# VectorE instead of GpSimd for every fourth weight subtraction in a two-block transformer kernel

## The chip, the cores and the metric

The kernel runs on one core of a Trainium2 chip. The metric is the device time of one execution in microseconds (us), taken as the median of several runs. The profile comes from one further execution, recorded by the hardware profiler.

## The reference

The input x is 256 tokens by 1024 features, in float32. Two blocks run one after the other.

- **First block.** `h = rms_norm(x)`, a projection `h @ w_in` of three kinds of attention (banded and dilated, sliding window with sinks, stick-breaking) and three gates, then `merged = sum of sigmoid(gate) * (o @ w_branch)`, `@ w_out`, a norm and a residual. After it a feed-forward part: `u = h @ w_up` (1024 to 8192), a causal convolution over three tokens, `gelu(gate) * val`, `@ w_down`, norm, residual.
- **Second block, two layers.** Each modulates a norm of x (and of a context of 256 tokens, in layer 0 to the end, in layer 1 only as far as attention needs it) with vectors `c_act @ ada_w`; projects with `w_in`; runs a chunked state-space scan (SSD) and a differential attention; merges both through `w_ssd_o`, `w_attn_o` and `w_out`; and adds `square(relu(h @ w1)) @ w2`, the MLP. A last norm ends it.

Nearly all arithmetic is in products of the form `h @ W` with 256 or 512 tokens, and all weights are float32.

## The kernel before

**Pieces.** Every weight matrix comes to SBUF in pieces of 128 partitions by 1024 float32 values (512 KB), each used for eight 128-row slices of one block of columns. `wload` (L194 to L214) handles one piece in three steps. A DMA on SyncE's queue brings it into `wr` (L202). ScalarE copies it to the reduced float32 format of TensorE, which gives its high part `wh` (L210). A subtraction gives the low part, `wl = wr - wh` (L213):

```python
nc.scalar.activation(hi, raw, AF.Copy)
self.nsplit += 1
eng = nc.gpsimd if self.nsplit % self.pool_every == 0 else nc.vector
eng.tensor_tensor(lo, raw, hi.bitcast(F32), op=ALU.subtract)
```

`nsplit` counts the pieces; `pool_every` is set stage by stage from the table `pv` or from constants: 4 in the first block, 8 for the SSD stages, 99 (next to none) in differential attention and one stretch of the MLP, 4 elsewhere. There are 578 pieces; 112 of the subtractions fall to GpSimd and 466 to VectorE.

**Products.** Activations are split into a high and a low part in the same way (`split`, L257; `h` of a modulated norm, L949). `mmT` (L220 to L232) then does three matmuls for each slice: L230 is high by high, L231 high by low, L232 the low part of the weight by the high part of the activation; `mmN` (L251 to L253) does the same with the operands exchanged. The slot of `wr` comes free when both parts have been made, the slots of `wh` (five) and `wl` (five) when the matmuls have read them.

**What sets the order.** TensorE's instructions run in the order in which the program writes them (`in_order`); generators are woven by hand, so that projections fill the gaps of attention or the scan. On the other engines a tile scheduler sets the order by priorities, before the run; each engine then takes its instructions strictly in that order and waits at the first whose operand isn't there. `wload` gives its three steps a priority that depends on when earlier pieces are used.

**Other names.** `sq` (L303) are sums of squares in `norm`. `rstd` turns them into the inverse root: VectorE's `rv` (L272), GpSimd's `rr` (L274), VectorE's diagonal `dg` (L278); TensorE spreads that over the partitions (L286, `sm`) and the norm is multiplied in on VectorE (L946). `acc` (L830) on VectorE is a tap of the convolution in the feed-forward part, it reads PSUM; `gv` (L835) on GpSimd is its gated product. L915 on VectorE are the dot products of the modulation vectors, with raw weights `wa` from the same buffers as `wr`. L1748 on VectorE adds a branch to the residual.

Of the kernel before, what the change touches and what calls it, by code (L numbers as in the profile page):

```python
# [10 lines left out]
F32 = mybir.dt.float32  # L11
F32R = mybir.dt.float32r
AF = mybir.ActivationFunctionType
ALU = mybir.AluOpType
# [84 lines left out]
class Net:  # L99
    def __init__(self, ctx, tc, A, stop=None, x_only=False):  # L100
        self.ctx, self.tc, self.nc, self.A = ctx, tc, tc.nc, A
        self.stop = stop
        p = lambda name, bufs, **k: ctx.enter_context(tc.tile_pool(name=name, bufs=bufs, **k))
        self.cp = p("cp", 1)
        self.NR, self.NH = 6, 5
        self.back = 4
        self.wr = p("wr", self.NR)
        self.wh = p("wh", self.NH)
        self.wl = p("wl", 5)
        self.ps_mm = p("psmm", 3, space=PSUM)  # L110
        self.ps_sm = p("pssm", 3, space=PSUM)
        self.ps_lg = p("pslg", 2, space=PSUM)
        self.sp = p("sp", 2)
        self.nsplit = 0
        self.HP = 100
        self.MW = 2
        self.H2 = 256
        self.XP = (1,3,5)
        self.GN = 4
        self.RP = 100  # L120
        self.pieces = []
        self.first = None
        self.pv = (4,4,4,8,99,4,4)
        self.pool_every = self.pv[0]
        self.FD = ({2:(0,),4:(1,),6:(2,),7:(3,)},{2:(0,),4:(1,),7:(2,3)})
        self.B0 = (5,5)
        self.WW = ((2,0,1),(2,0,2))
        self.NA = 12
        self.L = (3,2)
        self.L0 = (4,4)  # L130
        nc = self.nc
        self.cst = self.cp.tile([P, 6 * P], F32, name="cst")
        self.smt = self.cp.tile([P, NSM], F32, name="smt")
        self.row = self.cp.tile([P, NRW], F32, name="row")
        self.nhalf = self.cp.tile([P, 4], F32, name="nhalf")
        nc.vector.memset(self.nhalf, -0.5)
        warm = self.cp.tile([P, 4], F32, name="warm")
        nc.scalar.activation(warm, self.nhalf, AF.Copy)
# [55 lines left out]
    def wload(self, src, kt=8, eng=None):  # L194


        nc = self.nc
        shape = [P, kt, src.shape[1] // kt]
        now = self.tc.tile_snap_priority()
        with self.tc.high_priority(offset=0 if self.first is None else min(self.RP, max(0, now - self.first))):  # L200
            raw = self.wr.tile(shape, F32, tag="wr", name="wr")
            (eng or nc.sync).dma_start(raw, src.rearrange("p (k n) -> p k n", k=kt))  # L202

        turn = self.pieces[-self.back][0] if len(self.pieces) >= self.back else 0
        piece = [now]
        self.pieces.append(piece)
        with self.tc.high_priority(offset=0 if self.first is None else max(0, min(now - 1, now - turn))):
            hi = self.wh.tile(shape, F32R, tag="wh", name="wh")
            lo = self.wl.tile(shape, F32R, tag="wl", name="wl")
            nc.scalar.activation(hi, raw, AF.Copy)  # L210
            self.nsplit += 1
            eng = nc.gpsimd if self.nsplit % self.pool_every == 0 else nc.vector
            eng.tensor_tensor(lo, raw, hi.bitcast(F32), op=ALU.subtract)  # L213
        return [(hi[:, k, :], lo[:, k, :], piece) for k in range(kt)]  # L214

    def wload2(self, src):
# [124 lines left out]
    def first_block(self, es_x):  # L341


        nc, tc, A = self.nc, self.tc, self.A
        w_in = A["w_in"]
        xsrc = lambda k: A["xT"][k * P:(k + 1) * P, :]
        with ExitStack() as es:
# [410 lines left out]
            def context():  # L758
                for _ in range(8):
                    yield  # L760
                yield from self.mod_norm(0, 0, 1, xc, hc, 0, t1, nc.gpsimd if 1 else None)
                for k in range(8):
                    nc.sync.dma_start(hcd[k], hct[k].bitcast(F32))
# [8 lines left out]
            W2 = A["w_in_2"][0]  # L772
            with self.in_order():
                self.ada_finish(0, 0, 24)
                self.pool_every = self.pv[1]
                bg = [context()]
                self.weave(merge(), bg)
                self.weave(project(), bg)
                self.dump("d_hs", hs)

                free = []

                def t16():
                    if not free:
                        for c in range(4, 12):
                            t = pb.tile([P, 2, 256], F32, tag=f"gate{c}", name="t16")
                            free.extend((t[:, 0, :], t[:, 1, :]))
                    return free.pop(0)

                bg = [self.add_normed(x, hs, "post_g", t16)]  # L790
                self.step(bg)
                self.weave(self.gate_blocks(W2[72:76], hc, 0, 256, spill(t1)), bg)
                while bg:
                    self.step(bg)
                h = self.pairs(po, 8, 256, "o")
                bg = [self.normed(x, "ffn_g", t16, h)]
                self.step(bg)
                sink = spill(t1)
                self.weave(self.gate_blocks(W2[76:80], hc, 0, 256, lambda i, make: sink(4 + i, make)), bg)
                while bg:  # L800
                    self.step(bg)

        self.hp = self.side_pool(es_x, "hp", 8, "left")
        with ExitStack() as es:
# [41 lines left out]
                    else:  # L846
                        nc.vector.tensor_tensor(hs[c], pv_, hs[c], op=ALU.add)

            self.pool_every = self.pv[2]
            with self.in_order():  # L850
                for q in range(4):
                    mid = self.pairs(pm, 8, 256, "mid")
# [203 lines left out]
    def ssd_open(self, l, h):  # L1056

        class Phase:
            pass

        class Tags:
            def __init__(s_):
                s_.m = {}

            def tile(s_, shape, dt, tag, name):
                return s_.m[tag].tile(shape, dt, tag=tag, name=name)

        nc = self.nc
        S = Phase()
        S.es, S.tags, S.bg, S.times, S.fr, S.h = ExitStack(), Tags(), [], {}, {}, h  # L1070
        S.p4 = self.side_pool(S.es, f"s4{l}", 4, "right")
        S.p2 = self.side_pool(S.es, f"s2{l}", 3, "right")
        S.tags.m.update({"cv": S.p4, "bc": S.p4, "sz": S.p4, "s2": S.p2})
        p1 = self.side_pool(S.es, f"sc{l}", 1, "right")
        self.cwh = p1.tile([P, 160], F32, name="cwh")
        nc.vector.tensor_scalar(self.cwh, self.sm(f"cw{l}"), 0.5, None, op0=ALU.mult)
        self.cbh = p1.tile([P, 32], F32, name="cbh")
        nc.vector.tensor_scalar(self.cbh, self.sm(f"cb{l}"), 0.5, None, op0=ALU.mult)
        S.dT = S.p2.tile([64, 512], F32, tag="s2", name="dT")
        self.pool_every = (4,4)[l]  # L1080
        S.nv = (3,2)[l]
        S.vd = self.tc.dram_tile([S.nv, P, 512], F32, name=f"vd{l}")
        S.front = self.ssd_front(l, 0, h, S.fr, S.tags, S.dT, lambda: S.bg.append(S.start()))
        return S
# [377 lines left out]
    def layer(self, l, x, S):  # L1462

        nc, tc, A = self.nc, self.tc, self.A
# [2 lines left out]
        nt = T // P  # L1467
        W = A["w_in_2"][l]
        h = S.h
        self.pool_every = (8,8)[l]  # L1470
        yd = tc.dram_tile([16, P, T], F32, name=f"yd{l}")
        ad = tc.dram_tile([8, P, T], F32, name=f"ad{l}")
        gd = tc.dram_tile([8, P, T], F32, name="gd1") if last else self.gd
# [8 lines left out]
        with S.es as es:  # L1482
# [11 lines left out]
            fr, front = S.fr, S.front  # L1494
            for g in range(8):
                self.weave(front, bg)
                self.pool_every = self.pv[3]
                bg.append(self.ssd_back(l, g, fr, S.times, yd, ssq, pools))
                if g < 7:
                    fr = {}  # L1500
                    front = self.ssd_front(l, g + 1, h, fr, S.tags)
# [7 lines left out]
            while bg:  # L1509
                self.step(bg)  # L1510
        nc.vector.tensor_reduce(tot[:, :nt], ssq[:, :nt, :], axis=AX.X, op=ALU.add)
        self.pool_every = self.pv[4]
        es_m, es_x, es_p, es_g = ExitStack(), ExitStack(), ExitStack(), ExitStack()
        pg = pool(es_g, "g", 8, "right")
        gs = []
# [28 lines left out]
            while bg:  # L1544
                self.step(bg)
        pt = pool(es_m, "mt", 6, "left")
        self.pool_every = self.pv[5]
        px = pool(es_x, "xc", 1, "left")
        streams = [(0, x, 0)]
        if not last:  # L1550
# [14 lines left out]
        with self.in_order():  # L1565
# [51 lines left out]
            if last:  # L1617
                es_g.close()
                pr = pool(es_g, "raw", 1, "right")
                raw = [pr.tile([P, 2, 258], F32R, name=f"raw{k}") for k in range(8)]  # L1620
                raw = [(t[:, 0, :], t[:, 1, :]) for t in raw]
# [7 lines left out]
        if not last:  # L1629
            es_g.close()  # L1630
        es_p.close()
        self.pool_every = self.pv[6]
        with ExitStack() as es, self.in_order():
            pma = pool(es, "ma", 8, "left")
            es_e = ExitStack()
# [55 lines left out]
            if last:  # L1691
                self.step(bg)
                self.weave(up_raw(), bg)
                es_g.close()
            else:

                self.weave(up(0, range(4), 256, 512), bg)
                self.pool_every = 99
                self.weave(up(1, range(4), 256, 512), bg)
                while bg:  # L1700
                    self.step(bg)
                bg.append(adas())
                self.weave(up(0, range(4), 0, 256), bg)
                self.pool_every = self.pv[6]
            for e in range(1, 7):
                cols = (0, 256) if e == 1 and not last else (0, T)
                self.weave(up(e, range(2), *cols), bg)
# [166 lines left out]
```

## Time and profile before

| what | value |
|---|---|
| median of 3 runs | 2613.73 us |
| lowest and highest | 2606.41 and 2618.48 us |
| the profiled execution, its own time | 2611.19 us |
| its span in the trace | 2609.4 us |
| mean granted TensorE clock | 0.991 of full speed |

The span lies between the first and the last instruction that the trace shows; 1.8 us of the profiled execution's time lie around it. The engines are PE (TensorE's matmuls), PEld (its weight loads), DVE (VectorE), ACT (ScalarE), POOL (GpSimd) and SP (SyncE, which issues most DMAs). Of an engine that isn't the bottleneck, idle time costs nothing by itself.

### The profile page before, as it was taken

Reading aid. Unit: us, or ns where it says so; the run is one execution under the profiler, and the core shown is the slowest. Engines: PE = TensorE matmul, PEld = TensorE weight load, DVE = VectorE, ACT = ScalarE, POOL = GpSimd, SP = SyncE. Lnnn points to the kernel's source line nnn. Section 1 sums busy time; section 2 is a strip of 40 time slices with the busy share of each in tenths; the row PEclk is TensorE's granted clock in tenths of the full one; section 3 lists DMA queues with packets and bytes.
Section 4 is the critical chain, followed back from the end, with each engine's and each line's share of the span. In section 5 each row is a group of like instructions: output and inputs, shape, how many; then the busy total and the mean of one; then the engine's idle time right before and its main releaser. Section 6 shows DMA issues by size and latency. Waiting matters only on the chain.

```text
span 2609.4 us, 44555 instructions
## 1 busy us (share of the span) xinstructions
PE 2513.0 (96%) x16698; PEld 2263.5 (87%) x16698; DVE 1876.7 (72%) x2990; ACT 1423.7 (55%) x2722; POOL 875.5 (34%) x757
## 2 busy tenths in 40 slices
PE   7999899999999999999999899999999999999998
PEld 7899899998888888888879878789878888899998
DVE  7887776877577765777796886636777767778664
ACT  5654565564656564666434623335565546665654
POOL 3123533332455564210133311014365542212321
PEclk9999899999999999999999999999999999999999
DMA  7665665663434335322674556624444343355552
GB/s 258 219 222 206 205 214 183 209 218 131 140 121 130 127 120 167 107 95 75 221 255 138 195 193 232 203 97 146 150 142 135 114 160 132 104 189 201 171 186 98
DMA packets 179766, 431.27 MB, mean 165 GB/s; under 512 B 18884, under 2 KB 84610, under 8 KB 179294
## 3 DMA queue, kind: packets, MB, share of 16 engines
q1 hardware_dynamic: 176254, 424.26, 48.6%
q0 software_dynamic: 2720, 3.64, 0.5%
q8 instruction: 132, 2.16, 0.3%
q14 instruction: 84, 0.69, 0.1%
q10 hardware_dynamic: 576, 0.52, 0.1%
HBM read 406.82 MB, written 18.32 MB: 163 GB/s over the span
## 4 chain that ended last, share of the span: by engine, by line
PE 57%; DVE 14%; DMA 8%; issue 7%; POOL 6%; ACT 6%; SPq 1%; POOLq 0%; DVEq 0%; ACTq 0%
PE mm L230 14%; PE mm L231 14%; PE mm L232 14%; DMA wa<-in_adaT_dram 4%; DVE wl L213 3%; PE mm L251 2%; PE mm L252 2%; PE mm L253 2%; DVE th L915 2%; ACT wh L210 2%; DVE junk L915 1%; PE sm L1190 1%; PE sm L1266 1%; POOL E L1175 1%; PE sm L1253 1%
## 5 line engine op out<-in xcount | busy, mean ns | idle before, releaser
L210 ACT ACTIVATE wh<-wr 128x1024 fp32r<-128x1024 f32 x578 | 610.1, 1057 | 631.1 <-PE mm L231 487.7
L230 PE MATMUL mm<-h,wh 128*128 128x256 f32 (+1 forms) x2232 | 765.7, 343 | 16.7 <-ACT r L1648 7.0
L213 DVE TENSOR_TENSOR wl<-wr,wh 128x1024 fp32r<-128x1024 f32 x466 | 603.9, 1298 | 223.2 <-ACT wh L210 216.9
L231 PE MATMUL mm<-h,wh 128*128 128x256 f32 (+1 forms) x2232 | 744.5, 334 | 2.6 <-DVE h L949 1.4
L232 PE MATMUL mm<-h,wl 128*128 128x256 f32 (+1 forms) x2232 | 744.7, 334 | 0.0
L213 POOL TENSOR_TENSOR wl<-wr,wh 128x1024 fp32r<-128x1024 f32 x112 | 285.6, 2550 | 796.1 <-ACT wh L210 734.0
L230 PEld LDWEIGHTS mm<-h,wh 128*128 128x128 f32 x2232 | 422.4, 189 | 67.7 <-ACT r L1648 7.2
L231 PEld LDWEIGHTS mm<-h,wh 128*128 128x128 f32 x2232 | 422.5, 189 | 51.9 <-issue 5.7
L232 PEld LDWEIGHTS mm<-h,wl 128*128 128x128 f32 x2232 | 421.8, 189 | 43.1
L230 PE MATMUL mm<-mid,wh 128*128 128x256 f32 (+1 forms) x832 | 254.9, 306 | 4.3 <-DVE xc L1748 3.9
L231 PE MATMUL mm<-mid,wh 128*128 128x256 f32 (+1 forms) x832 | 254.9, 306 | 1.4 <-DVE mid L257 1.3
L232 PE MATMUL mm<-mid,wl 128*128 128x256 f32 (+1 forms) x832 | 254.4, 306 | 0.0
L251 PE MATMUL mm<-wh,h 128*128 128x256 f32 (+1 forms) x704 | 202.3, 287 | 2.6 <-DVE bc L1051 1.2
L252 PE MATMUL mm<-wl,h 128*128 128x256 f32 (+1 forms) x704 | 197.1, 280 | 0.0
L253 PE MATMUL mm<-wh,h 128*128 128x256 f32 (+1 forms) x704 | 197.0, 280 | 0.0
L230 PE MATMUL mm<-o,wh 128*128 128x256 f32 x592 | 168.0, 284 | 13.0 <-ACT wh L210 7.7
L230 PEld LDWEIGHTS mm<-mid,wh 128*128 128x128 f32 x832 | 156.8, 188 | 14.5 <-issue 4.5
L232 PE MATMUL mm<-o,wl 128*128 128x256 f32 x592 | 167.6, 283 | 0.9 <-DVE wl L213 0.9
L231 PE MATMUL mm<-o,wh 128*128 128x256 f32 x592 | 167.2, 282 | 0.0
L231 PEld LDWEIGHTS mm<-mid,wh 128*128 128x128 f32 x832 | 156.6, 188 | 10.1 <-DVE mid L257 2.0
L232 PEld LDWEIGHTS mm<-mid,wl 128*128 128x128 f32 x832 | 156.4, 188 | 8.2
L915 DVE SCALAR_TENSOR_TENSOR th<-wa,cb 128x1024 bf16<-128x1024 f32 x96 | 136.7, 1432 | 12.8 <-DMA wa<-in_adaT_dram 11.9
(373 smaller groups left out, 4960.9 us busy)
## 6 DMA issues: line engine op xcount, KB each, us to landing
wr<-in_w_in_dram SPq DMA_DIRECT2D x247, 512.0 KB, 3.6
wr<-in_w_mlp_dram SPq DMA_DIRECT2D x144, 512.0 KB, 4.2
wa<-in_adaT_dram SPq DMA_DIRECT2D x96, 512.0 KB, 4.4
wr<-in_w_up_dram SPq DMA_DIRECT2D x64, 512.0 KB, 4.3
wr<-in_w_out_dram SPq DMA_DIRECT2D x32, 512.0 KB, 3.5
wr<-in_w_down_dram SPq DMA_DIRECT2D x32, 512.0 KB, 4.2
wr<-in_w_ssd_o_dram SPq DMA_DIRECT2D x32, 512.0 KB, 3.7
E<-csd SPq DMA_DIRECT2D x24, 512.0 KB, 4.4
```

The lines of the kernel that those rows point to most:

```text
L210: nc.scalar.activation(hi, raw, AF.Copy)
L213: eng.tensor_tensor(lo, raw, hi.bitcast(F32), op=ALU.subtract)
L230: nc.tensor.matmul(ps, wh, xh, start=start and k == 0, stop=False)
L231: nc.tensor.matmul(ps, wh, xl, start=False, stop=False)
L232: nc.tensor.matmul(ps, wl, xh, start=False, stop=stop and k == n - 1)
L251: nc.tensor.matmul(ps, xh, wh, start=k == 0, stop=False)
L252: nc.tensor.matmul(ps, xh, wl, start=False, stop=False)
L253: nc.tensor.matmul(ps, xl, wh, start=False, stop=k == n - 1)
L915: nc.vector.scalar_tensor_tensor(junk, raw, 0.5, self.cb[:, s, :], op0=ALU.mult, op1=ALU.mult, accum_out=self.mods[l][:, 2 * i + m, s:s + 1])
L1175: nc.gpsimd.tensor_tensor(v, v, t, op=ALU.add)
L1190: nc.tensor.matmul(ps[:, d0:d1, :], BN[:, c, :], xw[:, d0:d1].rearrange("p d h e -> p d (h e)"), start=True, stop=True)
L1253: nc.tensor.matmul(ps[:, d0:d0 + n].rearrange("p d h e -> p d (h e)"), C[:, ck * P:(ck + 1) * P], H[ck][:, d0:d0 + n, :], start=True, stop ...
```

## The change

The choice of the engine goes. The subtraction of L213 is always VectorE's, and `nsplit`, `pool_every` and `pv` are removed everywhere. Line numbers after the change are lower by 5 to 15 (L213 is then L208, L278 is L273, L835 is L829, L830 is L824, L949 is L942, L1748 is L1733).

```diff
-        self.nsplit = 0
...
-        self.pv = (4,4,4,8,99,4,4)
-        self.pool_every = self.pv[0]
...
             nc.scalar.activation(hi, raw, AF.Copy)
-            self.nsplit += 1
-            eng = nc.gpsimd if self.nsplit % self.pool_every == 0 else nc.vector
-            eng.tensor_tensor(lo, raw, hi.bitcast(F32), op=ALU.subtract)
+            nc.vector.tensor_tensor(lo, raw, hi.bitcast(F32), op=ALU.subtract)
...
-                self.pool_every = self.pv[1]
...
-            self.pool_every = self.pv[2]
...
-        self.pool_every = (4,4)[l]
...
-        self.pool_every = (8,8)[l]
...
-                self.pool_every = self.pv[3]
...
-        self.pool_every = self.pv[4]
...
-        self.pool_every = self.pv[5]
...
-        self.pool_every = self.pv[6]
...
-                self.pool_every = 99
...
-                self.pool_every = self.pv[6]
```

TensorE's order is the same. On the other engines the scheduler places things anew. Three places show how.

The first is VectorE's queue in the norm ahead of the MLP of layer 0, between the residual's updates (`xl`) and the first modulated activations (`nt`, `h`). Before:

```order
L213 TENSOR_TENSOR wl<-wr,wh 128x1024
L1748 SCALAR_TENSOR_TENSOR xl_2746<-mm,mod_86,xl_2746 128x256
L272 TENSOR_SCALAR rv<-sm 128x2
L278 TENSOR_SCALAR dg<-cst,rr 128x128 x2
L1748 SCALAR_TENSOR_TENSOR xl_2748<-mm,mod_86,xl_2748 128x256
L946 TENSOR_TENSOR nt<-xc_14325,sm 128x256
L213 TENSOR_TENSOR wl<-wr,wh 128x1024
L949 TENSOR_TENSOR h<-nt,h 128x256
```

With the change:

```order
L208 TENSOR_TENSOR wl<-wr,wh 128x1024
L1733 SCALAR_TENSOR_TENSOR xl_2746<-mm,mod_86,xl_2746 128x256
L267 TENSOR_SCALAR rv<-sm 128x2
L273 TENSOR_SCALAR dg<-cst,rr 128x128 x2
L208 TENSOR_TENSOR wl<-wr,wh 128x1024
L1733 SCALAR_TENSOR_TENSOR xl_2748<-mm,mod_86,xl_2748 128x256
L939 TENSOR_TENSOR nt<-xc_14325,sm 128x256
L208 TENSOR_TENSOR wl<-wr,wh 128x1024
L942 TENSOR_TENSOR h<-nt,h 128x256
```

The moved subtraction stands behind the diagonals `dg`, not ahead of them; nothing new stands between `rv` and `dg`.

The second is VectorE's queue in the middle of the feed-forward part's up-projection, with the convolution's taps (`acc`). Before:

```order
L257 TENSOR_TENSOR mid<-gv,mid 128x256
L830 SCALAR_TENSOR_TENSOR acc<-mm,smt,acc 128x255
L830 SCALAR_TENSOR_TENSOR acc<-mm,smt,acc 128x254
L830 SCALAR_TENSOR_TENSOR acc<-mm,smt,acc 128x255
L830 SCALAR_TENSOR_TENSOR acc<-mm,smt,acc 128x254
L213 TENSOR_TENSOR wl<-wr,wh 128x1024
L257 TENSOR_TENSOR mid<-gv,mid 128x256
L213 TENSOR_TENSOR wl<-wr,wh 128x1024 x2
L830 SCALAR_TENSOR_TENSOR acc<-mm,smt,acc 128x255
```

With the change:

```order
L252 TENSOR_TENSOR mid<-gv,mid 128x256
L824 SCALAR_TENSOR_TENSOR acc<-mm,smt,acc 128x255
L824 SCALAR_TENSOR_TENSOR acc<-mm,smt,acc 128x254
L208 TENSOR_TENSOR wl<-wr,wh 128x1024
L824 SCALAR_TENSOR_TENSOR acc<-mm,smt,acc 128x255
L824 SCALAR_TENSOR_TENSOR acc<-mm,smt,acc 128x254
L208 TENSOR_TENSOR wl<-wr,wh 128x1024
L252 TENSOR_TENSOR mid<-gv,mid 128x256
L208 TENSOR_TENSOR wl<-wr,wh 128x1024 x2
L824 SCALAR_TENSOR_TENSOR acc<-mm,smt,acc 128x255
```

The moved subtraction stands between the taps of the two halves, and the second half's taps wait behind it.

The third is GpSimd's queue at the start of the feed-forward part. Before:

```order
L274 TENSOR_TENSOR rr<-rv,nhalf 128x2
L213 TENSOR_TENSOR wl<-wr,wh 128x1024
L814 DMA h<-hcd 128x2x256 x8
L213 TENSOR_TENSOR wl<-wr,wh 128x1024
L835 TENSOR_TENSOR gv<-acc 128x256
L213 TENSOR_TENSOR wl<-wr,wh 128x1024
L835 TENSOR_TENSOR gv<-acc 128x256 x2
```

With the change:

```order
L940 TENSOR_SCALAR t_3259<-t_3258,gsc_88,mod_86 128x256
L942 TENSOR_TENSOR hc<-t_3259,hc 128x256
L269 TENSOR_TENSOR rr<-rv,nhalf 128x2 x2
L808 DMA h<-hcd 128x2x256 x8
L829 TENSOR_TENSOR gv<-acc 128x256 x32
L269 TENSOR_TENSOR rr<-rv,nhalf 128x2
```

The 32 gated products follow one another with no subtraction between them, and nothing stands ahead of the eight DMAs but the norm's own work.

## Rows read from the trace of the kernel before

**Rows 1.** The page's first part: busy time, share of the span, instructions

```profile
PE 2513.0 (96%) x16698; PEld 2263.5 (87%) x16698; DVE 1876.7 (72%) x2990; ACT 1423.7 (55%) x2722; POOL 875.5 (34%) x757
```

**Rows 2.** The chain that ended last, by engine

```profile
PE 57%; DVE 14%; DMA 8%; issue 7%; POOL 6%; ACT 6%; SPq 1%; POOLq 0%; DVEq 0%; ACTq 0%
```

**Rows 3.** Waits of PE, whole span: us in total, times, longest

```profile
PE sm L286 <- DVE dg L278: 7.9, 8, 2.5
...
PE mm L230 <- DVE acc L830: 5.3, 5, 1.6
...
PE mm L232 <- DVE wl L213: 0.9, 1, 0.9
```

**Rows 4.** The instructions of L213: duration in ns (shortest/median/longest), first and last start

```profile
L213 DVE TENSOR_TENSOR wl<-wr,wh x466: 1207/1224/3417, 7.7 to 2585.4; 128x1024 fp32r<-128x1024 f32 x156
...
L213 POOL TENSOR_TENSOR wl<-wr,wh x112: 2353/2412/4422, 14.9 to 2579.8; 128x1024 fp32r<-128x1024 f32 x112
```

**Rows 5.** Timeline of the norm at 1425 us: start, us, instruction, [idle before, releaser]

```profile
1424.71 0.71 POOL L274 TENSOR_TENSOR rr<-rv,nhalf 128x2 f32<-128x2 f32 x1 [3.44 <-DVE rv L272]
...
1425.39 2.38 POOL L213 TENSOR_TENSOR wl<-wr,wh 128x1024 fp32r<-128x1024 f32 x1
1425.45 2.60 DVE L278 TENSOR_SCALAR dg<-cst,rr 128x128 f32<-128x128 f32 x2 [0.82 <-POOL rr L274]
```

**Rows 6.** The instructions of L278 and of L830, as in Rows 4

```profile
L278 DVE TENSOR_SCALAR dg<-cst,rr x30: 273/286/2409, 21.5 to 2601.8; 128x128 f32<-128x128 f32 x30
...
L830 DVE SCALAR_TENSOR_TENSOR acc<-mm,smt,acc x128: 465/481/484, 329.1 to 571.0; 128x255 f32<-128x255 f32 x64, 128x254 f32<-128x254 f32 x64
```

**Rows 7.** Timeline: the first and the last held instruction of VectorE, and its holder

```profile
14.91 4.42 POOL L213 TENSOR_TENSOR wl<-wr,wh 128x1024 fp32r<-128x1024 f32 x1 [2.82 <-ACT wh L210]
...
17.22 2.39 DVE L303 TENSOR_TENSOR sq<-sq 128x256 f32<-128x256 f32 x1
...
2568.16 2.41 POOL L213 TENSOR_TENSOR wl<-wr,wh 128x1024 fp32r<-128x1024 f32 x1 [8.89 <-ACT wh L210]
...
2569.23 1.62 DVE L257 TENSOR_TENSOR mid<-r,mid 128x256 fp32r<-128x256 f32 x1 [2.40 <-ACT mid L256]
```

**Rows 8.** Timeline at 337 us: a subtraction on GpSimd beside two convolution taps

```profile
337.03 2.40 POOL L213 TENSOR_TENSOR wl<-wr,wh 128x1024 fp32r<-128x1024 f32 x1 [3.79 <-ACT wh L210]
...
337.52 1.00 DVE L830 SCALAR_TENSOR_TENSOR acc<-mm,smt,acc 128x255 f32<-128x255 f32 x2 [0.64 <-ACT acc L827]
```

**Rows 9.** Windows of 16 places: us, busy PE PEld DVE ACT POOL, PEclk, DMA, GB/s

```profile
16.50:20.00 3.50, 1.48 (x14) 1.40 (x14) 3.01 (x3) 1.93 (x2) 2.83 (x1) 1.00 1.04 371
...
288.00:297.00 9.00, 6.08 (x47) 6.00 (x46) 6.71 (x9) 5.77 (x11) 2.63 (x3) 0.84 0.89 329
...
1344.00:1351.00 7.00, 4.46 (x16) 3.36 (x16) 7.00 (x7) 2.69 (x3) 4.43 (x2) 0.85 0.92 310
...
2431.00:2437.00 6.00, 5.03 (x43) 4.83 (x42) 5.72 (x7) 4.89 (x13) 2.65 (x1) 1.00 0.72 236
sum 95.20, PE 72.96 PEld 65.64 DVE 86.50 ACT 47.17 POOL 51.28; mean PE 4.56 PEld 4.10 DVE 5.41 ACT 2.95 POOL 3.20
```

**Rows 10.** Waits of all engines, whole span

```profile
POOL wl L213 <- ACT wh L210: 734.0, 85, 23.8
ACT wh L210 <- PE mm L231: 487.7, 272, 8.5
DVE wl L213 <- ACT wh L210: 216.9, 177, 5.5
```

**Rows 11.** Window of the feed-forward part, columns as in Rows 9

```profile
330.00:600.00 270.00, 264.70 (x2268) 263.84 (x2267) 196.58 (x282) 157.32 (x237) 88.34 (x55) 1.00 0.60 203
```

**Rows 12.** The same window, instructions of L213 alone: busy DVE, POOL

```profile
330.00:600.00 270.00, 96.62 (x72) 57.95 (x23) 1.00 0.60 203
```

**Rows 13.** Waits in the same window

```profile
DVE wl L213 <- ACT wh L210: 38.6, 35, 4.1
...
POOL wl L213 <- ACT wh L210: 66.5, 22, 8.5
```

## The prediction

> **What bounds the kernel now.** I read the page's totals first. TensorE's matmuls are busy for 2513.0 of 2609.4 us, 96%, and VectorE for 72% [rows 1]; so the kernel can gain at most 96.4 us from anything that isn't a matmul, and its weight path is not starved: in the whole span TensorE waits once, for 0.9 us, for a low part [rows 3]. The chain that ended last is TensorE for 57%, VectorE for 14% and GpSimd for 6% [rows 2]; of the two engines that the change touches, VectorE is the one that is often the last to be waited for. Then the waits of TensorE: the larger ones on VectorE are for the norms' diagonals `dg`, 7.9 us in 8 times, and for the convolution's `acc`, 5.3 us in 5 [rows 3].
>
> Next I looked at what the two kinds of the subtraction cost their engines. VectorE takes 1.22 us, GpSimd 2.41 us [rows 4], and the timeline of a norm shows something that the totals hide. `rr` ends at 1425.42, and VectorE begins its two diagonals at 1425.45; GpSimd has begun a subtraction at 1425.39, and the pair, which takes 2 x 0.286 us elsewhere [rows 6], takes 2.60 us and ends only behind it [rows 5]. So a subtraction on GpSimd **holds** an instruction of VectorE, which counts as busy meanwhile. I listed every VectorE instruction that overlaps one of the 112 and took longer than the shortest tenth of its kind: 62 of the 112 held one, the first `sq` at 17.22 us (2.39 us), the last `mid` at 2569.23 [rows 7], 103 us in all. Those held read two operands from SBUF or are of the diagonals' kind. The convolution's taps, which read PSUM, never were: none of 128 took over 0.484 us [rows 6], also with a subtraction beside them [rows 8].
>
> The Trainium skill ("SBUF — State Buffer", section "Who interferes with whom") says that VectorE and GpSimd share a pair of ports, that an instruction of VectorE with two SBUF inputs contends for it with a GpSimd instruction that reads SBUF, and that the one that begins first keeps it to its end. The trace agrees in kind; if all 112 had held VectorE for all of their 2.41 us, it would be 270 us, and the sum for VectorE would be a gain of 133 us in place of the loss below. The count of 62 decides.
>
> **What the change does.** It takes 112 subtractions from GpSimd and gives VectorE 112 x 1.224 = 137 us of work, and takes away 103 us of holds. VectorE is thus loaded with 34 us more, 1.3% of the span: from 72% to about 73%. That alone moves nothing. What counts is where, so I make two terms.
>
> *Term A, the holds that reached TensorE (gain).* TensorE begins an instruction more than 0.35 us late within 6 us of a held instruction at 16 places. Over windows drawn around these, TensorE is busy for 72.96 of 95.20 us [rows 9], so 22.2 us idle, 1.39 us a place. By the new order, 7 of the 16 have no subtraction put directly ahead of the instruction that was held; the norm's diagonals are one (first pair of orders). I count those in full: 7 x 1.39 = 9.7 us. At the other 9 a new subtraction stands there, and 1.22 us of work take the place of a hold of up to 2.1 us (2.60 less twice 0.286 is 2.0 [rows 5, 6]); I count 0.9 us each, 8 us. Together 18 us. Bounds: 0, if what TensorE waited for at these places was late anyway, as at 16.5 us, where the DMA engines are as full as the window shows (1.04); and 22.2, all of it. At two of the places the granted clock is 0.84 and 0.85 [rows 9], a part of the time at the 1.2 GHz level, behind idle stretches of TensorE; if those stretches go, matmuls of 6.08 and 4.46 us gain some 16%, 1.7 us, which I take only into the upper bound: 24 us.
>
> *Term B, work where there was no hold (cost).* 112 less 62 are 50 subtractions that disturbed nobody. Each is now 1.22 us in VectorE's queue, 61 us. And each can wait there: VectorE's own waited for ScalarE's high part for 216.9 us over 466 [rows 4, 10], 0.47 us each, so 23 us more for 50. What is queued behind it waits too: taps, `mid`, the norms' products, and through them TensorE. How much of VectorE's work ends up in the end time I take from the chain, 14% [rows 2]: 84 x 0.14 = 12 us. Bounds: 0, if all of it falls into VectorE's 28% of idle time, and 19 us, if all 137 us count at 14%.
>
> *What I cost at nothing.* `wl` itself being made earlier or later: its cover is that ScalarE, not the subtraction, sits waiting for TensorE to free a `wh`, 487.7 us in 272 times [rows 10], so pieces are mostly made ahead of their use; without that cover it is the 0.9 us of [rows 3] that grows. GpSimd's queue: its subtractions waited 734.0 us in 85 times [rows 10], with `gv`, `rr` and eight DMAs behind them, and that goes (third pair of orders); where it delayed TensorE it lies in term A's windows or ended in another engine's wait, and I add nothing. SyncE's queue: the weight DMAs change order in the first 230 us, because the slots of `wr` come free in another order; with the same cover I price this at nothing too.
>
> **Sum**, against the profiled execution's own 2611.2 us (2.5 under the median of the three runs): 2611.2 - 18 + 12 = **2605 us**, 0.3% below the median. Its own range, with either term off by half, is about 2595 to 2617.
>
> **Rivals.**
> - *Full gain.* All of term A with its clock, and VectorE's idle time takes all of term B: 2611.2 - 24 = 2587 us. For it: VectorE is idle in every stage and its load grows by 1.3% only. Against: at 9 of 16 places a new subtraction stands directly ahead.
> - *VectorE becomes the bound in the feed-forward part (slower).* From 330 to 600 us TensorE is busy for 264.7 of 270 [rows 11]; nothing can be gained there, and 23 of GpSimd's subtractions move [rows 12], among taps that they never held. If a moved one waits on VectorE as it did on GpSimd, 66.5 / 22 = 3.0 us [rows 13], and blocks the taps behind it (second pair of orders), 23 x (3.0 + 1.22) = 97 us stand against 270 - 196.6 = 73.4 us of idle time [rows 11]: 24 us over, 2605 + 24 = 2629 us; with nothing of term A, 2647. It decides from a wait of 73.4 / 23 - 1.22 = 2.0 us on. For it: five of TensorE's waits are for just these taps [rows 3], and a wait at the head of a strict queue is what GpSimd could afford and VectorE can't. Against: VectorE's own 72 waited 38.6 us there, 0.54 each [rows 12, 13].
> - *Nothing happens.* The holds and the work offset each other, as 103 and 137 us nearly do, and the 16 places are late for other reasons: 2611 us. The Trainium skill ("Perfetto Trace Analysis", "Optimizing Scalar/DVE Operations") says that moving work to GpSimd may make sense where VectorE is saturated but that between these two it might not help, since they share a port. By it, taking the offload back costs nothing where VectorE isn't saturated, and the trace shows it at 72%.
>
> **How the numbers follow.** Chances: the sum 0.42, full gain 0.20, VectorE as the bound 0.26, nothing 0.12. I give the slower case more than its row alone would, since a wait at the head of VectorE's queue is the one cost that I could only take by analogy. A difference of under 0.5% (13 us, so 2601 to 2627) can't be told from none here, as the three runs spread over 12 us. Of the sum's 0.42 some 0.08 lie below 2601. Faster: 0.20 + 0.08 = 0.28; slower: 0.26; the same: 0.34 + 0.12 = 0.46. The range of 8 in 10 reaches from 2587, the full gain, to 2636, which leaves out half of that case and the upper third of the slower one.
>
> **What would show it.** In the new profile: no VectorE `dg` over 0.3 us, and TensorE's wait for `dg` down from 7.9 to about 2 us (term A); VectorE busy for about 1911 us (137 less 103); waits of `wl` for `wh` on VectorE up from 217 to about 270 us (term B). From 330 to 600 us, a stage as long as before says that VectorE has room; one that is 15 us longer or more, with TensorE's wait for `acc` well above 5.3 us, says that the second rival is right. I would be wrong in the other direction if the places of term A stayed as long as they are: then another engine, or the DMA, was late there, and the hold only stood in front of it.

## The result, and the profile after

The change made the kernel faster: 2586.16 us median (2582.36 to 2593.39, 4 runs) against 2616.11 us before (4 runs), a ratio of 0.9886, 95% interval [0.9867, 0.9905]. That is 0.8 us under the low end of the forecast range, and the direction was not forecast. The profiled execution has a span of 2580.6 us, 28.8 us less than before.

The page's first part of the kernel after, and the chain that ended last:

```profile
PE 2507.5 (97%) x16698; PEld 2264.1 (88%) x16698; DVE 1900.0 (74%) x3102; ACT 1423.5 (55%) x2722; POOL 600.0 (23%) x645
...
PE 73%; issue 10%; DVE 6%; ACT 5%; POOL 3%; DMA 3%; SPq 1%; POOLq 0%; DVEq 0%; ACTq 0%
```

Against [rows 1], VectorE has 112 instructions more but only 23 us more of busy time. Its instructions' durations add up to 36 us more, since 137 us of subtractions came and the holds by those 112, some 102 us, went; the busy time counts stretches in which two of its instructions overlap only once, and these grew too. VectorE does more, and its share of the chain [rows 2] falls from 14% to 6%.

The instructions of the subtraction (now L208) and of the norm's diagonals (now L273), in ns (shortest/median/longest):

```profile
L208 DVE TENSOR_TENSOR wl<-wr,wh x578: 1205/1225/2247, 7.9 to 2556.8; 128x1024 fp32r<-128x1024 f32 x193
...
L273 DVE TENSOR_SCALAR dg<-cst,rr x30: 279/285/537, 20.7 to 2573.2; 128x128 f32<-128x128 f32 x30
```

The longest diagonal falls from 2409 to 537 ns [rows 6]; that one, at 305.9 us, stands beside two of GpSimd's DMA issues (L808). The timeline of the norm that [rows 5] showed at 1425 us, now at 1407:

```profile
1406.34 0.71 POOL L269 TENSOR_TENSOR rr<-rv,nhalf 128x2 f32<-128x2 f32 x1 [3.44 <-DVE rv L267]
...
1407.08 0.48 DVE L273 TENSOR_SCALAR dg<-cst,rr 128x128 f32<-128x128 f32 x2 [0.82 <-POOL rr L269]
1407.48 1.22 DVE L208 TENSOR_TENSOR wl<-wr,wh 128x1024 fp32r<-128x1024 f32 x1
```

The pair of diagonals takes 0.48 us where it took 2.60, and the moved subtraction comes behind it. Waits of the whole span, and the window of the feed-forward part (columns as in [rows 9]):

```profile
PE sm L281 <- DVE dg L273: 4.5, 4, 2.5
...
PE mm L227 <- DVE wl L208: 1.3, 2, 0.9
...
DVE wl L208 <- ACT wh L207: 268.8, 239, 5.4
```

```profile
321.20:586.30 265.10, 265.10 (x2268) 265.10 (x2267) 210.37 (x305) 156.99 (x237) 31.88 (x32) 1.00 0.61 207
```

TensorE's list has no wait for the convolution's `acc` any more (5.3 us before [rows 3]). Nor has it one for the residual `xc`, which before was

```profile
PE mm L230 <- DVE xc L1748: 3.9, 3, 2.2
```

The feed-forward part, the same 2268 matmuls as in [rows 11], takes 265.1 us where it took 270, and TensorE is busy throughout.

**Where the 28.8 us came from.** TensorE runs the same 16,698 matmuls in the same order, so the two traces can be lined up matmul by matmul; the difference of their start times at two points says what the stretch between gained. In us, by the times of before:

| 0–250 | 250–330 | 330–600 | 600–1240 | 1240–1440 | 1440–1860 | 1860–2160 | 2160–end |
|---|---|---|---|---|---|---|---|
| +1.0 | -9.9 | -4.9 | -0.7 | -4.5 | -12.3 | +3.3 | -1.0 |

The gain lies in the norms and in the stretches in which VectorE also makes the modulation vectors (L908, once L915). Each trace is a single execution: in stretches in which the kernels give the same work to the same engines, traces of e7_ffn (below) and of the kernel after differ by up to 3.3 us, so the small entries tell nothing. Summed over the 16 windows of [rows 9] alone it is 22.3 us, practically all that TensorE idled there (22.2). The clock came back with it: the stretches of the windows at 288 and 1344 us have a granted clock of 1.00, and their matmuls are busy for 5.24 and 3.40 us in place of 6.08 and 4.46.

Outside the windows the largest gains are at matmuls that waited for `acc` and `xc`. All five waits for `acc` between 330 and 600 us are gone, 6.1 us when lined up; four of them lie outside the windows, 8 to 27 us behind the last held instruction, and the three for `xc` (4.4 us) lie 10 to 33 us behind. One of them before the change, on GpSimd, VectorE and TensorE:

```profile
484.46 2.47 POOL L213 TENSOR_TENSOR wl<-wr,wh 128x1024 fp32r<-128x1024 f32 x1 [4.11 <-ACT wh L210]
...
484.59 3.42 DVE L915 SCALAR_TENSOR_TENSOR th<-wa,cb 128x1024 bf16<-128x1024 f32 x1
...
490.73 0.47 DVE L830 SCALAR_TENSOR_TENSOR acc<-mm,smt,acc 128x254 f32<-128x254 f32 x1
...
491.84 1.00 DVE L830 SCALAR_TENSOR_TENSOR acc<-mm,smt,acc 128x255 f32<-128x255 f32 x2 [0.64 <-ACT acc L827]
...
492.99 0.36 PE L230 MATMUL mm<-o,wh 128*128 128x256 f32 x1 [1.19 <-DVE acc L830]
```

The held `th` takes 3.42 us where others take 1.22. VectorE has next to no idle time from there to 491.2 us, so the taps behind it, which nothing held, come late, and TensorE waits for one 8 us after the hold began.

### The profile page after: what moved, and what is told of

It is laid out like the page before. It is cut to its first block, busy times and chain, and to the rows that moved or that the text cites. A ratio compares the mean times of both kernels' runs of the same rounds, so it can differ in the third digit from the quotient of the medians.

```text
span 2580.6 us, 44520 instructions
## 1 busy us (share of the span) xinstructions
PE 2507.5 (97%) x16698; PEld 2264.1 (88%) x16698; DVE 1900.0 (74%) x3102; ACT 1423.5 (55%) x2722; POOL 600.0 (23%) x645
## 4 chain that ended last, share of the span: by engine, by line
PE 73%; issue 10%; DVE 6%; ACT 5%; POOL 3%; DMA 3%; SPq 1%; POOLq 0%; DVEq 0%; ACTq 0%
PE mm L225 19%; PE mm L226 19%; PE mm L227 19%; PE mm L246 2%; PE mm L247 2%; PE mm L248 2%; PE sm L1258 1%; PE sm L1182 1%; ACT wh L207 1%; DVE wl L208 1%; DMA ru<-qk 1%; PE sm L1245 1%; SPq L1312 1%; PE lg L1401 1%; POOL nt L940 1%
## 5 line engine op out<-in xcount | busy, mean ns | idle before, releaser
L208 DVE TENSOR_TENSOR wl<-wr,wh 128x1024 fp32r<-128x1024 f32 x578 | 733.2, 1271 | 281.4 <-ACT wh L207 268.8
L225 PE MATMUL mm<-h,wh 128*128 128x256 f32 (+1 forms) x2232 | 765.0, 343 | 12.3 <-ACT r L1635 7.0
L246 PEld LDWEIGHTS mm<-wh,h 128*128 128x128 f32 x704 | 135.1, 192 | 3.6 <-ACT bc L1038 1.2
L247 PEld LDWEIGHTS mm<-wl,h 128*128 128x128 f32 x704 | 135.2, 192 | 0.6
```

The costliest lines, as they stand in the source:

```text
L208: nc.vector.tensor_tensor(lo, raw, hi.bitcast(F32), op=ALU.subtract)
L225: nc.tensor.matmul(ps, wh, xh, start=start and k == 0, stop=False)
L246: nc.tensor.matmul(ps, xh, wh, start=k == 0, stop=False)
L247: nc.tensor.matmul(ps, xh, wl, start=False, stop=False)
```

## The experiments

Each was timed in interleaved runs with the kernel before; ratios are to it. "Held" is the time by which VectorE's instructions beside the GpSimd work in question exceed the shortest tenth of their kind; by this count the kernel before has 102 us, in 60 instructions. Holds by GpSimd's other work are not in the table: counted over all of GpSimd's instructions they are 172 us before and 67 us after, so some 70 us of them stay. "Busy" is VectorE's, of the profiled execution. The kernel before, timed with each group of kernels, had medians from 2615 to 2619 us, so medians of different groups can differ by 3 us for that alone; the ratios are free of it.

Four kernels (e9_none, e11_none_set, e12_none_own, e13_unread) do not compute the reference. For the 112 pieces their third matmul takes the high part in place of the low one, so it adds the large part of the product a second time; their recorded expectations call that leaving out a small part, which is wrong. TensorE's work is the same in number and shape.

| kernel | median us | ratio [95%] | busy | held |
|---|---|---|---|---|
| before | 2616 | 1 | 1877 | 102 |
| after | 2586.2 | 0.9886 [0.9867, 0.9905] | 1900 | 0 |
| e1_tiny | 2580.3 | 0.9871 [0.9850, 0.9892] | 1898 | 0.7 |
| e2_hold | 2680.2 | 1.0242 [1.0219, 1.0265] | 2050 | 162 |
| e3_dve2 | 2614.3 | 0.9994 [0.9978, 1.0010] | 2022 | 0 |
| e4_half | 2602.7 | 0.9940 [0.9917, 0.9963] | 1882 | 47 |
| e5_own | 2640.2 | 1.0072 [1.0055, 1.0089] | 1980 | 86 |
| e6_memset | 2604.4 | 0.9941 [0.9925, 0.9957] | 1896 | 2.7 |
| e7_ffn | 2602.3 | 0.9939 [0.9923, 0.9955] | 1887 | 20 |
| e8_rope | 2586.1 | 0.9869 [0.9846, 0.9892] | 1901 | 0 |
| e9_none | 2572.2 | 0.9838 [0.9824, 0.9851] | 1771 | 0 |
| e10_quarter | 2602.2 | 0.9948 [0.9935, 0.9960] | 1825 | 50 |
| e11_none_set | 2577.7 | 0.9856 [0.9840, 0.9872] | 1769 | 1.7 |
| e12_none_own | 2591.9 | 0.9907 [0.9887, 0.9927] | 1840 | 71 |
| e13_unread | 2608.9 | 0.9974 [0.9962, 0.9986] | 1877 | 109 |

**e1_tiny, e2_hold: GpSimd's queue or the hold?** VectorE makes all low parts, and GpSimd makes a copy that nobody uses, of 8 columns or of all 1024 (`n`). The order of the other engines stays nearly that of the kernel after.

```diff
+            nc.vector.tensor_tensor(lo, raw, hi.bitcast(F32), op=ALU.subtract)
+            if self.nsplit % self.pool_every == 0:
+                f = lambda t: t.rearrange("p k n -> p (k n)")[:, :n]
+                nc.gpsimd.tensor_tensor(self.scr[:, :n], f(raw), f(hi.bitcast(F32)), op=ALU.subtract)
```

> The kernel after the change, with an extra GpSimd subtraction of only 128x8 values, into a scratch tile, at each of the 112 pieces that GpSimd had before. It computes the reference in full, the extra result is not used. GpSimd's queue has its old order and waits for the same high parts, but VectorE is hardly held, and makes all low parts. Theory H (the gain comes from VectorE no longer being held by long subtractions): about 2586 us, within 6, holds by these extras under 10 us. Theory Q (the gain comes from GpSimd's own work no longer standing behind subtractions that wait for the high part): back to about 2610 us. Theory S (the gain comes from the new order on VectorE, which this kernel shares with the one after): 2586 us.

> As the one before, but the extra GpSimd subtraction has the full 128x1024 values (into a scratch tile that nobody reads, in an 8-bit format). It computes the reference in full. VectorE makes all low parts in the order of the kernel after the change and is held as in the kernel before. Theory H: the 29 us come back and VectorE's larger load may add to them: 2612 to 2635 us, with about 60 holds of 100 us in all. Theory Q: about 2610 us, no more than with 128x8 values. Theory S: 2586 us, within 6, whatever the holds.

The waits of GpSimd came back for the most part in e1_tiny (659.8 us for the high part, 734.0 before [rows 10]), and the time did not go back: 2580.3 us, within what theory H gave. So its own work standing behind such waits (theory Q) was not what cost. With the full width the time rose by 94 us over the kernel after, 45 us above the range expected; the instruction with the 8-bit output took longer (3.39 us median), so this price is that of a larger dose. Theory S falls with it: all but some 50 of VectorE's 3102 instructions stand in the order of the kernel after, in both kernels.

**e5_own, e6_memset: buffers, or any work on GpSimd?** Behind the 128x8 subtraction GpSimd works on the scratch tile alone, once reading it and once only writing it.

```diff
+                nc.gpsimd.tensor_tensor(self.scr, self.scr, self.scr, op=ALU.subtract, saturate=False)
```

```diff
+                for _ in range(8):
+                    nc.gpsimd.memset(self.scr[:, :].bitcast(F32), 0.0)
```

> The kernel after the change with the 128x8 extra of e1_tiny at each of the 112 pieces (to wait for the same high part) and behind it a full 128x1024 GpSimd subtraction whose operands are the scratch tile itself. It computes the reference in full. So VectorE can be held as in e2_hold, but the buffers of the piece are not read any longer by it. Theory H (a hold of VectorE costs, at the 0.58 us for each us held that e2_hold showed, 94 of 162): 2640 to 2680 us, with 110 to 160 us of holds. Rival R (late release): e2_hold was slow because GpSimd's long reader gave the slots of the raw and the high part back late; without that 2580 to 2590 us, whatever the holds.

> As e5_own, but in place of the long subtraction eight GpSimd memsets of the scratch tile, which read nothing from SBUF and keep GpSimd busy for some 2 us. It computes the reference in full. If VectorE is held by what GpSimd reads (the rule in the Trainium skill, "SBUF - State Buffer", "Who interferes with whom"): hardly a hold, 2578 to 2590 us. If any long work on GpSimd disturbs VectorE or GpSimd's own later work: 2600 us or more.

The instructions of GpSimd's extra and of the diagonals, e5_own:

```profile
L219 POOL TENSOR_TENSOR scr<-scr x112: 1892/1899/2967, 19.1 to 2620.2; 128x1024 fp8e4<-128x1024 fp8e4 x112
...
L284 DVE TENSOR_SCALAR dg<-cst,rr x30: 275/286/1996, 21.7 to 2640.9; 128x128 f32<-128x128 f32 x30
```

and e6_memset:

```profile
L220 POOL MEMSET scr<- x896: 301/312/604, 18.9 to 2572.5; 128x256 f32 x180
...
L285 DVE TENSOR_SCALAR dg<-cst,rr x30: 278/286/477, 22.1 to 2590.7; 128x128 f32<-128x128 f32 x30
```

The longest diagonal is as long as the reading GpSimd instruction beside it (1996 beside 1899; 2409 beside 2412 in the kernel before), and beside memsets there is no such hold. With reads of tiles that no other instruction needs, the time rises by 54 us over the kernel after, so the late release of buffers isn't needed for the loss (rival R falls as the cause of all of it). The time lies at the low edge of theory H's range, with 86 us of holds where 110 to 160 were expected. The second expectation failed in part: there is hardly a hold, as the rule has it, but the time is in the range of the other case, since the memsets still cost 18 us (14 by the ratios). So the clean price of the holds is e5_own against e6_memset, which were timed together and keep GpSimd busy for 946 and 970 us: 83 us more of holds, 36 us more time, 0.4 us each.

**e3_dve2, e9_none: what does the moved work cost?** VectorE makes the 112 low parts twice, or not at all.

```diff
+            if self.nsplit % self.pool_every == 0:
+                nc.vector.tensor_tensor(self.scr, f(raw), f(hi.bitcast(F32)), op=ALU.subtract, saturate=False)
```

```diff
+            lo = hi
+            if self.nsplit % self.pool_every:
+                lo = self.wl.tile(shape, F32R, tag="wl", name="wl")
+                nc.vector.tensor_tensor(lo, raw, hi.bitcast(F32), op=ALU.subtract)
```

> As the two before, but the extra full subtraction at the 112 pieces is VectorE's: it makes these low parts twice, the second time into a scratch tile. It computes the reference in full. It prices the moved work itself, 112 x 1.22 = 137 us of VectorE without any hold. If work on VectorE costs the 14% that the prediction took from the chain: 2586 + 19 = 2605 us. If VectorE's idle time takes it: 2586 us, within 6. If VectorE is at its bound in stretches (the feed-forward part, the modulation vectors): 2615 us or more, with waits of TensorE for the convolution's taps.

> The kernel after the change without the 112 subtractions that moved: for these pieces no low part is made, and the third matmul reads the high part again (this leaves out a small part of each such product; TensorE's work is the same in number and shape). It prices the moved work with nothing in its place. If work on VectorE costs what e3_dve2 showed (28 us for 137 us): 2586 - 28 = 2558 us. By the prediction's 14%: 2567 us. If VectorE's idle time had taken it: 2586 us, within 6.

Without the 112 subtractions the time is 2572.2 us; made on VectorE they cost 14 us; made a second time, another 28. Neither kernel came out at a value expected for it: e3_dve2 lies between the 14% and the bound, e9_none between the 14% and nothing. The price of VectorE's time isn't one number: the second 137 us cost about twice what the first did (28 and 13 us by the ratios, each within some 6). Whether that is VectorE's larger load (1900 to 2022 us busy) alone isn't shown, since the second reading also gives the raw and high parts back later and the scheduler's order changes. From e9_none the kernel before lies 1.62% of 2616, or 42 us away: that is what the same subtractions cost on GpSimd.

**e4_half, e10_quarter, e7_ffn: dose, length and place.** Half as many pieces; each of GpSimd's subtractions cut into four; GpSimd only from the merge to the end of the feed-forward part. Of the first and the third edit one line is shown; the constants elsewhere change with it (doubled, or 999).

```diff
-        self.pv = (4,4,4,8,99,4,4)
+        self.pv = (8,8,8,16,99,8,8)
```

```diff
+                for i in range(0, 1024, 256):
+                    nc.gpsimd.tensor_tensor(f(lo, i), f(raw, i), f(hi.bitcast(F32), i), op=ALU.subtract)
```

```diff
-        self.pv = (4,4,4,8,99,4,4)
+        self.pv = (999,4,4,999,999,999,999)
```

> The kernel before with every interval doubled (8 for 4, 16 for 8): about 56 subtractions stay on GpSimd. Theory H: about half of the holds, some 50 us, and half of the gain: 2600 us, 2594 to 2607. Theory S (another order on VectorE): no fixed relation, it could lie anywhere from 2586 to 2616. Theory Q: also about half, 2600 us, with GpSimd's waits for the high part at about 370 us.

> The kernel before, with each of GpSimd's 112 subtractions cut into four of 128x256 values; all other engines keep exactly their order. It computes the reference in full. If a hold lasts as long as the one GpSimd instruction that stands in the way (0.6 us in place of 2.4): holds by these fall from 102 to some 30 to 50 us and the time to 2586 to 2600 us, at VectorE's smaller load perhaps below the kernel after. If VectorE stays held until the whole piece is done, or GpSimd's occupancy is what costs: 2610 us or more.

> The kernel before, with GpSimd making every fourth low part only from the first block's merge to the end of its feed-forward part (30 of the 112), and VectorE all others. By lining up TensorE's instructions of the two kernels one by one, those after the change run 15 us ahead between 240 and 600 us. If the gain is made where the holds are: 2586 + 15 = 2601 us, 2595 to 2607. If the prediction's second rival were right in direction (VectorE short of room in this stretch): below 2586 us.

Half the pieces give 47 us of holds and about half the gain, as theory H said (theory Q said the same time, so this alone doesn't part them). The cut pieces take 0.742 us each; the longest diagonal in this kernel:

```profile
L217 POOL TENSOR_TENSOR wl<-wr,wh x448: 717/742/1891, 15.7 to 2575.1; 128x256 fp32r<-128x256 f32 x150
...
L282 DVE TENSOR_SCALAR dg<-cst,rr x30: 280/286/777, 20.6 to 2594.2; 128x128 f32<-128x128 f32 x30
```

So a hold lasts as long as the one GpSimd instruction in the way. Holds fall by 52 us and the time by 14 us, though GpSimd is busy for longer (990 us, 875.5 before); VectorE, ScalarE and GpSimd's other work stand exactly in the order of the kernel before, so a changed order isn't the cause. The time lies just above what was expected for it and doesn't beat the kernel after. e7_ffn came out where the alignment put it: 30 subtractions between 240 and 600 us cost 16 us (14 by the ratios).

**e8_rope: less of the holds that remain.** GpSimd's rotary operations and one addition go to VectorE as well.

```diff
-            nc.gpsimd.tensor_tensor(t[:, :256], t[:, :256], self.rope[:, :256], op=ALU.mult)
-            nc.gpsimd.tensor_tensor(t[:, :256], t[:, :256], u, op=ALU.add)
+            nc.vector.tensor_tensor(t[:, :256], t[:, :256], self.rope[:, :256], op=ALU.mult)
+            nc.vector.tensor_tensor(t[:, :256], t[:, :256], u, op=ALU.add)
...
-                            nc.gpsimd.tensor_tensor(acc[i], acc[i], gs[i], op=ALU.add)
+                            nc.vector.tensor_tensor(acc[i], acc[i], gs[i], op=ALU.add)
```

> The kernel after the change with three more kinds of GpSimd work moved to VectorE: the two rotary operations on qk (64 instructions) and the addition to acc in the SSD output projection (16). It computes the reference in full. In the kernel after, these hold VectorE for 27.3 us. At 0.57 us for each us held and 0.205 for each us of added work (the prices of e2_hold and e3_dve2; 36 us of work): 15.6 - 7.4 = 8 us less, 2578 us, 2573 to 2584. If holds cost no more than work, or the stretch is bound by other things: 2586 us or more.

The median is that of the kernel after; the ratio's interval holds both 2578 and 2586 us. It doesn't tell, and it shows no gain; whether prices taken from one place carry to another stays open.

**e11_none_set, e12_none_own, e13_unread: dividing the 42 us.** The first two are e9_none with GpSimd kept busy as in e6_memset and e5_own; the third is the kernel before with

```diff
+            if self.nsplit % self.pool_every == 0:
+                lo = hi
```

so that GpSimd's results are not read.

> As e9_none (the 112 low parts are not made, the third matmul reads the high part for these pieces), with GpSimd doing at each of them a 128x8 subtraction, which waits for the high part, and eight memsets of a scratch tile that read nothing: GpSimd is as busy as before, VectorE does no more than before and should not be held. If GpSimd's own later work, delayed by that, cost the 18 us by which e6_memset lies above the kernel after: 2572 + 18 = 2590 us. If that was an effect of VectorE's larger load in e6_memset: 2572 to 2578 us.

> As e11_none_set (112 low parts left out, the high part read instead), with one full GpSimd subtraction of the scratch tile from itself in place of the memsets: GpSimd is as busy as before within a third, and VectorE can be held. If the kernel before lost its time to holds and to GpSimd's occupancy together: between e11_none_set and 2616 us, with 70 to 100 us of holds, each us of them worth 0.3 to 0.45 us above e11_none_set: 2610 to 2625 us. If GpSimd's own delay was all of it: the same as e11_none_set, or less, as GpSimd is busy for less long.

> The kernel before, in which GpSimd still makes its 112 low parts from the same buffers and for as long, but nobody reads them: the third matmul reads the high part for these pieces (this leaves out a small part of each such product). If the kernel before lost time because TensorE, or the buffers of the low part, waited for GpSimd's later results: well under 2616 us, near the 2592 us of e12_none_own, 2588 to 2602. If holds, GpSimd's occupancy and the late release of raw and high parts are all of it: 2610 to 2618 us, with about 100 us of holds.

GpSimd's occupancy adds 5 us to e9_none, as expected if e6_memset's loss hung on VectorE's larger load, and the intervals of the two overlap. In e12_none_own 69 us more of holds add 14 us more, 0.2 us each; 0.3 to 0.45 and 2610 to 2625 us were expected, so that expectation failed. Not having to wait for GpSimd's results takes 7 us off the kernel before (ratio 0.9974, so 4 to 10 us); at 2608.9 us it lies between its two ranges, 1 us under the higher one.

TensorE's waits for `acc` and `xc` come and go with the holds. They are 9.2 us before, none after, 0.7 in e9_none, 2.1 in e6_memset, 16.3 in e5_own and 6.5 in e12_none_own, whose lines are:

```profile
PE mm L238 <- DVE xc L1756: 4.2, 3, 2.9
...
PE mm L238 <- DVE acc L838: 2.3, 2, 1.9
```

So of the 42 us some 5 are occupancy, 7 are low parts that come late, and the other 30 are what is left: holds, with the late release of the raw and high parts in them, 0.3 us for each of 102 us held. At the 0.2 of e12_none_own the holds alone would be 20. How much of the 30 is release was not separated. The division also takes it that these pieces add up, which isn't shown: the scheduler placed some instructions of VectorE and ScalarE elsewhere in e9_none and e13_unread.

## Why the prediction was wrong

- **Direction of most steps: right.** Holds by the 112 go, the median diagonal is 0.285 us (the longest 0.54, none over 0.3 forecast), VectorE's busy time came to 1900 us (1911 forecast) and its waits for the high part to 268.8 us (about 270 forecast). TensorE's wait for diagonals fell to 4.5 us, not 2.
- **The failing step: the size of term A.** It read "Together 18 us. Bounds: 0 [...] and 22.2, all of it", or 24 with the clock. Measured, taking the subtractions from GpSimd gives back 42 us (e9_none against before), of which the holds with the late release are some 30. Two things were wrong. At 9 of the 16 places I counted 0.9 us because a new subtraction stands there; but the 16 windows gained 22.3 us net of those subtractions. And I took the idle time within 6 us of held instructions for the whole, where a hold also reaches TensorE later, through VectorE's queue: lined up, e9_none gains 25 us in the 16 windows and 36 in all, 8 of them between 330 and 600 us, where the prediction said that nothing can be gained. Of these 8, 6 are the five waits for `acc`, and only one of the five lies in a window.
- **Term B: right in size.** 12 us forecast, 14 measured (2586.2 less 2572.2; 13 by the ratios). That was in part luck: the 14% of the chain happened to fit, and e3_dve2 shows that the next 137 us cost twice as much.
- **Costed at nothing.** `wl` being late was worth some 7 us (e13_unread), though TensorE waited only 0.9 us for it by name [rows 3]. GpSimd's own delayed work cost nothing that shows where it only waited (e1_tiny), 5 us where it was busy (e11_none_set, not clear of noise), and 14 to 18 us with VectorE's larger load (e6_memset). Why the last two differ, by 10 us within some 8 by the ratios, stays open.
- **The rivals.** "Full gain" named the time, 2587 us, but not the reason, so that it came so near is luck: VectorE's idle time did not take term B, and term A was larger than its bound. VectorE did not become the bound in the feed-forward part: 95 subtractions there waited 34.3 us in 48 times, 0.36 us each, where 2.0 would have decided; the analogy with GpSimd's waits failed, and why those were longer was not tested. "Nothing happens" is out.
- **The rule on the shared ports**, which the prediction took from the Trainium skill ("SBUF — State Buffer", "Who interferes with whom"), agrees with e6_memset and e10_quarter: beside memsets there is hardly a hold (2.7 us in all), beside reading subtractions there is, and it lasts for one instruction (0.777 us at most for a diagonal beside pieces of 0.742).

## What to carry to other kernels

Before giving work to a second engine, look at whether instructions of the first one grow longer beside it: here 112 subtractions cost 14 us on VectorE, busy for 74%, and 42 us on GpSimd, busy for 34%. A held microsecond strikes an instruction that was ready, and what it delays can stand 8 us or more behind it, so don't price it by the idle time next to it; line up the two kernels' TensorE instructions, and run a kernel without the work at all, which tells about how much a better placement can still give (here 14 us).

## What the runs showed of the hardware that was not expected

The hold goes both ways. GpSimd's subtraction of 128x8 values in e1_tiny takes 0.20 us at the shortest, but 1.19 us in the median and up to 3.89:

```profile
L216 POOL TENSOR_TENSOR scr<-wr,wh x112: 200/1187/3890, 14.7 to 2550.1; 128x8 fp8e4<-128x8 f32 x112
```

One of them in e6_memset, on GpSimd and on VectorE:

```profile
1405.26 1.24 POOL L218 TENSOR_TENSOR scr<-wr,wh 128x8 fp8e4<-128x8 f32 x1 [1.05 <-ACT wh L213]
...
1407.51 2.53 POOL L220 MEMSET scr<- 128x256 f32 x7
```

```profile
1405.22 1.23 DVE L215 TENSOR_TENSOR wl<-wr,wh 128x1024 fp32r<-128x1024 f32 x1 [0.54 <-ACT wh L213]
...
1408.05 1.23 DVE L215 TENSOR_TENSOR wl<-wr,wh 128x1024 fp32r<-128x1024 f32 x1 [0.54 <-ACT wh L213]
```

VectorE begins 0.04 us earlier, and GpSimd's 8 columns end with VectorE's 1024; seven memsets beside the next subtraction leave it at 1.23 us.
